# Output projection and first gate as plain products, and the rooms of SBUF in three zones

## The chip, the cores and the metric

The kernel runs on one core of one Trainium2 chip. The metric is the device time of one execution in microseconds; the median of three runs is shown below, and beside it one execution taken with the hardware profiler. The engines are TensorE (PE; its weight loads are PEld), VectorE (DVE), ScalarE (ACT), GpSimd (POOL) and SyncE (SP, which issues most DMAs). Each works through its own queue in order and waits on semaphores for the others.

## The reference

A decoder of two layers on one sequence of 1024 tokens, model width 1024, all in float32. Cut to what matters here:

```python
for i in range(DEPTH):                                  # 2 layers
    u = rms_norm(h, attn_norm_w[i])
    proj = u @ w_in[i]                                  # all heads' inputs
    fox = forgetting_attention(...)                     # 8 heads of 64, causal softmax with forget gates
    ret = silu(rg) * head_group_norm(chunkwise_retention(...))   # 8 heads of 64
    mixed = jnp.concatenate([fox, ret], axis=-1)
    h = h + mixed @ w_out[i]                            # output projection, 1024 x 1024
    h = h + gated_conv_ffn(rms_norm(h, ffn_norm_w[i]), w_up[i], conv_w[i], conv_b[i], w_down[i])
    gate = jax.nn.sigmoid(rms_norm(h, ple_norm_w[i]) @ w_ple_gate[i])   # gate, 1024 x 1024
    h = h + gate * (p[i] @ w_ple_proj[i])
return rms_norm(h, final_norm_w)
```

## The kernel before, in words

Activations lie with features on the 128 partitions and the 1024 tokens along the free axis, so a vector of 1024 features is eight tiles of 128x1024. A float32 product is made of three passes on TensorE: every operand is split into a high part (a cast to fp32r) and a low part (the rest), and high x high, low x high and high x low are summed in PSUM. ScalarE casts the high part (`wh`, `xh`, `dh`, `uh`), VectorE or GpSimd subtracts for the low one (`wl`, `xl`, `dl`, `ul`).

There are two ways to multiply. The *plain* one (`dense_fm`) makes one block of 128 output features from eight tiles of 128 input features: 8 x 3 x 2 matmuls of 128x512, 48 in all, and one result `d` of 128x1024. The *seven-product* one (`g_parts`) treats 256 inputs by 256 outputs by two halves of the tokens as a 2x2 block product and makes it with seven products where eight would be needed (names `b0 c1 b1 c2 b2 a b3`). For it the weights are combined: `Fixed` loads two raw tiles `wr`, GpSimd adds them to `ws`, ScalarE and VectorE split them in four stages. The moving side is combined too: `Joined` makes four stages (`x`, `xh`, `xl`) from two tiles with VectorE's help (`t2`, `t34`). Each of the seven results is added to its quarter by `join` (sums into h) or `form` (new tiles). `Line` keeps one set of weights in preparation while the one before is used: after parts 0, 2, 4 and 6 one step of the next is issued. The second and later parts of `b` and `c` go into the same PSUM bank on top of the first, after the first has been read.

The program of a layer: the input projections of the heads are plain. `weave` mixes their steps with units of attention by the numbers in `SPANS` (position at which a unit starts and should end, in microseconds of dense work); four pairs of fox heads come first, then four pairs of retention heads. The dense work in order is `DENSE`; its last entry `wo0` (`g_out`) is the first half of the output projection, that of the fox heads, beside the last retention unit. When all units are done the second half follows, then the up projection with convolution (11 bodies, each two `g_parts` a and z), the down projection (four groups), and the gate. In layer 0 the output projection, up, down and gate use seven products; the gate of layer 1 is plain. h goes to DRAM between stages and comes back by DMA. Plain weights come through `weight_order`, `fetch` and `weights`, one set ahead, and `load_w` splits them on the engine that `ENGINES` names.

All large tiles live in one arena of 50 rooms of 128x1024 and 6 of half the size. `take` gives the room that has been free longest, `back` puts it at the end of the queue; a new holder's first write must wait until the old holder's last reader is done. The order of instructions on each engine is then set by a scheduler from these dependencies.

The lines shown in the profile as L145 are one helper through which every operation passes, so in the rows the names of tiles tell operations apart: `h<-h,d` is a join, `a` and `z` are the two results of an up body, `conv` its convolution, `sg` the gate.

Of the kernel before, what the change touches and what calls it, by code (L numbers as in the profile page):

```python
# [9 lines left out]
F32 = mybir.dt.float32  # L10
# [7 lines left out]
DEPTH = 2  # L18
# [17 lines left out]
DENSE = ("fi1", "rv0", "fi2", "fv1", "fi3", "ri0", "rv1", "rg0", "ri1", "ri2", "rg1", "ri3", "ep0", "em0", "wo0")  # L36
SPANS = ((6, 42.6), (42.6, 79.9), (85.9, 123.5), (130.4, 145.5), (138.9, 199.2), (194.7, 197.7), (217.3, 254.5), (251.1, 300.0))
# [3 lines left out]
ROOMS = 50  # L41
HALVES = 6
# [59 lines left out]
class Arena:  # L102


    def __init__(self, tc, pool, whole, half):
        self.tc, self.pool = tc, pool
        self.free = {T: deque("m%d" % i for i in range(whole)), T // 2: deque("n%d" % i for i in range(half))}
        self.taken = []
        self.first = {}

    def back(self, room):
        self.taken.remove(room.name)
        self.free[T if room.place[0] == "m" else T // 2].append(room.place)

    def take(self, name, dt, shape):
        free = self.free[T if int(np.prod(shape[1:])) > T // 2 else T // 2] or self.free[T]
        if not free:
# [42 lines left out]
def trunk(ctx, tc, ap):  # L160
# [4 lines left out]
    arena = Arena(tc, sb, ROOMS, HALVES)  # L165
# [43 lines left out]
    def weight_order():  # L209
        V, G_ = nc.vector, nc.gpsimd  # L210
        for l in range(DEPTH):
            qk = lambda j: (ap["wqk"][l, j], KC, P, E("qk", j))
            tm = lambda j: [(ap["wtm"][l, j, i], 4, 256, E("tm", 2 * j + i)) for i in range(2)]
            fv0 = [(ap["wfv"][l][:, a:b, :], b - a, FVW, G_) for a, b in FVK]
            specs = {"ep": lambda i: [], "wo": lambda i: [],
                     "fi": lambda i: [qk(i), qk(4 + i)], "fv": lambda i: tm(0), "ri": lambda i: [qk(8 + i), qk(12 + i)],
                     "rv": lambda i: tm(1 + i), "rg": lambda i: tm(3 + i),
                     "em": lambda i: [(ap["wproj"][l, j], 8, P, E("em", j)) for j in range(2)]}
# [693 lines left out]
    for l in range(DEPTH):  # L912
# [120 lines left out]
        def hand(now, then):  # L1033

            def after(n):
                for m in now:
                    m.drop(n)
                for m in then:
                    m.build(n)
            return after  # L1040

        def specs():
            for half in range(2):
                for q in range(4):
                    yield ap["wout"][l, half, q], 2
# [6 lines left out]
            if l + 1 < DEPTH:  # L1052
                for q in range(4):
                    yield ap["wgate"][l, q], 4

        def g_out():

            nonlocal line, u, rb
            u = rb = None
            del pr[:], ret_tab[:]  # L1060
            line = Line(specs())
            for p in range(2):
                mx.append(Joined(mixed[2 * p], mixed[2 * p + 1]))
                mixed[2 * p:2 * p + 2] = [None, None]
            for q in range(4):
                for m in (2 * q, 2 * q + 1):
                    h[m] = G("h")
                    nc.sync.dma_start(h[m], h_dram[m])
                to = h[2 * q:2 * q + 2]
                yield from g_parts(line, mx, lambda name, s: join(name, s, to))  # L1070

        fox_ops, ret_ops, ret_v, ret_tab, vst, tail = {}, {}, {}, [], [], []
        pr, mx, h, line = [], [], [None] * KC, None
        pp = dr.tile([KC, P, T], F32, name="pp")
        raw = []
        for name in ("qs", "ks"):
# [3 lines left out]
            if name == "qs":  # L1080
# [9 lines left out]
                  "em": lambda i: g_embed(), "wo": lambda i: g_out()}  # L1090
# [6 lines left out]
        del vst[:]  # L1097


        def scales(which, p):  # L1100
            return nw[:, which, 2 * p:2 * p + 1], nw[:, which, 2 * p + 1:2 * p + 2], minus[:, which, 2 * p + 1:2 * p + 2]

        stats = Stats()
        mx = [Joined(mixed[2 * p], mixed[2 * p + 1]) for p in (2, 3)]
        mixed = None
        u = []
        hs_dram = dr.tile([KC, P, T], F32, name="hs")
        for q in range(4):
            to = h[2 * q:2 * q + 2]
            parts(line, mx, lambda name, s: join(name, s, to), hand(mx, []) if q == 3 else None)  # L1110
            u.append(Joined(*to, scales(2 * NW_FFN + l, q)))
            for m in (2 * q, 2 * q + 1):
                stats.add(h[m], G("hsq"))
                nc.sync.dma_start(hs_dram[m], h[m])
                h[m] = None
        to = None
# [51 lines left out]
        for g, mx in enumerate(stored):  # L1168
            then = stored[g + 1] if g + 1 < len(stored) else []
            for q in range(4):  # L1170
# [9 lines left out]
                def after(n):  # L1180
                    for m in mx:
                        m.drop(n)
                    for m in then:
                        m.build(n)
                        if n < 3:
                            m.load(n + 1)
                    if not then and not ends:
                        u[2].build(n)
                parts(line, mx, lambda name, s: join(name, s, to), after if q == 3 else None)
                if not then:  # L1190
                    if ends:
                        u += [make_u(h[m], nw[:, 2 * NW_PLE + l, m:m + 1]) for m in (2 * q, 2 * q + 1)]
                    else:
                        u.append(Joined(*to, scales(2 * NW_PLE + l, q), q != 2))
                    for m in (2 * q, 2 * q + 1):
                        stats.add(h[m], G("hsq"), None, E("hsq", m))
                        if not ends:
                            nc.sync.dma_start(hs_dram[m], h[m])
                if not then and not ends:

                    for m in range(2 * q - 2 if q == 3 else 2 * q, 2 * q + 2):
                        if q != 2:
                            h[m] = None
# [3 lines left out]
        if not ends:  # L1207
            nstats = Stats()
            h_dram = dr.tile([KC, P, T], F32, name="hd")
            rb = None  # L1210
            old, u = u, []
            for q in range(4):
                sg = [G("sg") for i in range(2)]
                for m in (2 * q, 2 * q + 1):
                    h[m] = G("h")
                    nc.sync.dma_start(h[m], hs_dram[m])

                def scale_s(i):
                    nonlocal rb, stats
                    if rb is None:  # L1220
                        _, rb = stats.finish()
                        stats = None
                    return rb

                def after(n):
                    for m in old:
                        m.drop(n)
                    if n:
                        u.extend(make_u(h[m], nw[:, 2 * NW_ATTN + l + 1, m:m + 1]) for m in (2 * n - 2, 2 * n - 1))
                    if n == 2:  # L1230
                        fetch()
                parts(line, old, lambda name, s: form(name, s, sg, scale_s), after if q == 3 else None)
                for i in range(2):
                    m = 2 * q + i
                    pt = G("ppt")
                    nc.sync.dma_start(pt, pp[m])
                    nc.scalar.activation(sg[i], sg[i], AF.Sigmoid)
                    nc.gpsimd.tensor_tensor(sg[i], sg[i], pt, op=ALU.mult)
                    nc.vector.tensor_tensor(h[m], h[m], sg[i], op=ALU.add)
                    if q == 3:  # L1240
                        u.append(make_u(h[m], nw[:, 2 * NW_ATTN + l + 1, m:m + 1]))
                    nstats.add(h[m], sg[i])
                    nc.sync.dma_start(h_dram[m], h[m])
                    if q == 3:
                        h[m] = None
                sg = pt = None
            stats, nstats = nstats, None
            h = rb = old = None

    fetch()  # L1250
# [127 lines left out]
```

## Time and profile before

| what | value |
|---|---|
| median of 3 runs | 2899.47 us (2892.65 to 2899.89) |
| the profiled execution | 2898.59 us |
| its span (first to last instruction) | 2896.8 us |
| TensorE busy | 2717.5 us, 94%, 13718 matmul records |
| VectorE busy | 2086.6 us, 72% |
| ScalarE busy | 1226.5 us, 42% |
| GpSimd busy | 902.0 us, 31% |
| mean granted TensorE clock | 0.970 |

A record is one matmul instruction as the profiler saw it; a float32 matmul that isn't split has two. Matmuls overlap, so the mean duration of one (about 400 ns) isn't the time it takes out of the stream; the distance from one to the next is. Busy shares over the whole span mix stages that different engines limit, so the tables by stretches matter more.

### The profile page before, as it was taken

The page shows a single profiled execution, that of the slowest core. Times are in us where ns is not written, and L with a number is a line of the kernel's source. Part 1 is how long each engine was busy: PE and PEld are TensorE (multiplying, and loading weights), DVE is VectorE, ACT ScalarE, POOL GpSimd, SP SyncE. Part 2 cuts the span into 40 slices and gives each one's busy share as a digit, 9 for nine tenths or more (in the row PEclk, how much of TensorE's full clock was granted, in tenths as well). Part 3 has the DMA queues.
Part 4 walks back from the last instruction along what each step waited for, and adds up shares of the span by engine and source line. Part 5 has one row for each costly group of instructions (what it writes and reads, how often), then busy time and mean ns, then how long its engine had stood idle before and what let it go on. Part 6 is the DMA issues. An engine that isn't in the chain of part 4 may idle for free. (4 is left out here: it accounts for less than half of the span.)

```text
span 2896.8 us, 36327 instructions
## 1 busy us (share of the span) xinstructions
PE 2717.5 (94%) x13718; PEld 2263.5 (78%) x13718; DVE 2086.6 (72%) x3031; ACT 1226.5 (42%) x1824; POOL 902.0 (31%) x652
## 2 busy tenths in 40 slices
PE   8988999978999998997889989999799999989998
PEld 7887989757888887775678879897578888867776
DVE  4565645898887778779745556458978877787786
ACT  4354543444344333435434545424443433434352
POOL 3222332223233323434432222322232333234240
PEclk9999999999999999998989999999999999999999
DMA  5333122422323236433533331224223232364242
GB/s 161 88 81 95 54 61 71 158 76 95 109 99 113 95 132 213 153 95 120 178 91 88 81 97 52 62 72 154 77 95 109 99 112 96 137 208 151 87 146 98
DMA packets 116864, 315.77 MB, mean 109 GB/s; under 512 B 13520, under 2 KB 34512, under 8 KB 116688
## 3 DMA queue, kind: packets, MB, share of 16 engines
q1 hardware_dynamic: 113616, 305.05, 32.4%
q10 hardware_dynamic: 3072, 8.39, 1.2%
q8 instruction: 108, 1.77, 0.3%
q14 instruction: 68, 0.56, 0.1%
HBM read 210.04 MB, written 69.80 MB: 97 GB/s over the span
## 5 line engine op out<-in xcount | busy, mean ns | idle before, releaser
L145 POOL TENSOR_TENSOR ws<-wr 128x512 f32<-128x512 f32 (+2 forms) x192 | 285.7, 1495 | 1049.6 <-PE d L145 520.6
L145 PE MATMUL s<-xh,wh 128*128 128x512 f32 x936 | 377.8, 406 | 25.6 <-ACT wh L145 13.2
L145 PE MATMUL d<-xh,wh 128*128 128x512 f32 x936 | 374.8, 404 | 20.2 <-DVE h L145 12.6
L145 PE MATMUL s<-xl,wh 128*128 128x512 f32 x936 | 377.4, 403 | 11.2 <-DVE xl L145 11.2
L145 PE MATMUL s<-xh,wl 128*128 128x512 f32 x936 | 372.0, 403 | 6.1 <-DVE wl L145 5.7
L145 PE MATMUL d<-xl,wh 128*128 128x512 f32 x936 | 373.6, 399 | 2.4 <-DVE xl L145 2.4
L145 PE MATMUL d<-xh,wl 128*128 128x512 f32 x936 | 370.6, 399 | 0.0
L145 POOL TENSOR_TENSOR ws<-ws,wr 128x512 f32<-128x512 f32 (+2 forms) x192 | 262.9, 1370 | 104.2 <-issue 55.6
L145 PE MATMUL d<-x,w 128*128 128x512 f32 x936 | 246.2, 399 | 22.4 <-ACT x L145 8.8
L145 ACT CAST wh<-ws 128x1024 fp32r<-128x1024 f32 (+2 forms) x192 | 168.5, 888 | 219.8 <-POOL ws L145 203.6
L145 DVE TENSOR_TENSOR wl<-ws,wh 128x1024 fp32r<-128x1024 f32 (+2 forms) x192 | 218.3, 1146 | 40.7 <-ACT wh L145 31.9
L145 PE MATMUL d<-dh,uh 128*128 128x256 f32 (+1 forms) x768 | 222.1, 290 | 22.8 <-DVE vst L145 11.2
L145 PEld LDWEIGHTS s<-xh,wh 128*128 128x128 f32 x936 | 180.0, 192 | 76.3 <-ACT wh L145 20.5
L145 PEld LDWEIGHTS d<-xh,wh 128*128 128x128 f32 x936 | 178.9, 191 | 71.5 <-DVE h L145 21.0
L145 PEld LDWEIGHTS d<-x,w 128*128 128x128 f32 x936 | 175.3, 190 | 71.1 <-ACT x L145 10.1
L145 PEld LDWEIGHTS s<-xl,wh 128*128 128x128 f32 x936 | 180.5, 193 | 54.8 <-DVE xl L145 14.3
L145 PEld LDWEIGHTS s<-xh,wl 128*128 128x128 f32 x936 | 180.0, 192 | 54.5 <-DVE wl L145 13.3
L145 PE MATMUL d<-dl,uh 128*128 128x256 f32 (+1 forms) x768 | 221.8, 289 | 0.0
L145 PE MATMUL d<-dh,ul 128*128 128x256 f32 (+1 forms) x768 | 220.8, 288 | 0.0
L145 PE MATMUL d<-uh,dh 128*128 128x512 f32 (+1 forms) x584 | 197.6, 407 | 18.1 <-ACT dh L145 11.1
L145 PEld LDWEIGHTS d<-xl,wh 128*128 128x128 f32 x936 | 179.6, 192 | 43.7 <-DVE xl L145 3.0
L145 PEld LDWEIGHTS d<-xh,wl 128*128 128x128 f32 x936 | 178.9, 191 | 42.2
(209 smaller groups left out, 5863.3 us busy)
## 6 DMA issues: line engine op xcount, KB each, us to landing
wr<-in_wup_dram SPq DMA_DIRECT2D x88, 512.0 KB, 3.8
zz<-zd SPq DMA_DIRECT2D x66, 512.0 KB, 3.7
wr<-in_wdown_dram SPq DMA_DIRECT2D x48, 384.0 KB, 4.2
zd<-z SPq DMA_DIRECT2D x66, 256.0 KB, 2.0
dr<-in_wqk_dram SPq DMA_DIRECT2D x32, 512.0 KB, 3.5
hs<-h SPq DMA_DIRECT2D x24, 512.0 KB, 2.6
h<-hs SPq DMA_DIRECT2D x24, 512.0 KB, 4.8
zd<-t SPq DMA_DIRECT2D x22, 512.0 KB, 3.9
```

The source lines that it names most:

```text
L145: ins = f(*[bare(v) for v in a], **{n: bare(v) for n, v in k.items()})
```

## The change

The output projection of both layers and the gate of layer 0 become plain: one block of 128 outputs after the other with `dense_fm`, from weights in a plain layout that `weight_order` now delivers (`wout`, `wgate`). All eight tiles of mixed are split once, after the weave; no part of the projection is left in the weave, so the last retention unit ends at position 259.3 instead of 300. The moving sides of the up projection are still `Joined`, made after every second block. The next layer's moving sides are made in the gate, block by block. The arena has zones: 28 rooms for moving sides, 9 for split weights, 13 for the rest, 6 halves; a tile looks in its own zone first, then in r, w, x.

```diff
-DENSE = (... "ri3", "ep0", "em0", "wo0")
-SPANS = (... (217.3, 254.5), (251.1, 300.0))
+DENSE = (... "ri3", "ep0", "em0")
+SPANS = (... (217.3, 254.5), (251.1, 259.3))
-ROOMS = 50
-HALVES = 6
+ZONES = dict(x=28, w=9, r=13, n=6)
+HOMES = dict(x=("x", "xh", "xl", "uh", "ul", "mxh", "mxl", "qq", "ka", "kb"), w=("w", "wh", "wl", "dh", "dl"))
...
     def take(self, name, dt, shape):
-        free = self.free[T if int(np.prod(shape[1:])) > T // 2 else T // 2] or self.free[T]
+        home = next((z for z, names in HOMES.items() if name in names), "r")
+        zones = [home] + [z for z in "rwx" if z != home]
+        if int(np.prod(shape[1:])) <= T // 2:
+            zones.insert(0, "n")
+        free = next((self.free[z] for z in zones if self.free[z]), None)
...
+            yield from [(ap["wout"][l, m], KC, P, E("wo", m)) for m in range(KC)]
             yield None
-            for i in range(len(PIECES) if l + 1 == DEPTH else 0):
-                yield from [(ap["wlast"][0, m], KC, P, E("gate%d" % l, i * KC + m)) for m in range(KC)]
+            for i in range(len(PIECES) if l + 1 == DEPTH else 1):
+                yield from [(ap["wgate"][l, m], KC, P, E("gate%d" % l, i * KC + m)) for m in range(KC)]
...
+        mx = []
+        for c in range(8):
+            mx.append((G("mxh", F32R), G("mxl", F32R)))
+            split(*mx[c], mixed[c], E("mx", c))
+            mixed[c] = None
...
-        for q in range(4):
-            to = h[2 * q:2 * q + 2]
-            parts(line, mx, lambda name, s: join(name, s, to), hand(mx, []) if q == 3 else None)
-            u.append(Joined(*to, scales(2 * NW_FFN + l, q)))
...
+        for m in range(KC):
+            h[m] = G("h")
+            nc.sync.dma_start(h[m], h_dram[m])
+            if m == 4:
+                line = Line(specs())
+            elif m > 4:
+                line.step()
+            d = dense_fm(weights(), mx)
+            nc.vector.tensor_tensor(h[m], d, h[m], op=ALU.add)
+            nc.sync.dma_start(hs_dram[m], h[m])
+            stats.add(h[m], G("hsq"))
+            if m % 2:
+                u.append(Joined(h[m - 1], h[m], ...))
...
-                parts(line, old, lambda name, s: form(name, s, sg, scale_s), after if q == 3 else None)
+            for m in range(KC):
+                pt = G("ppt")
+                nc.sync.dma_start(pt, pp[m])
+                d = dense_fm(weights(), u)
+                if m == 0:
+                    _, rb = stats.finish()
+                sg = G("sg")
+                if m < 2:
+                    nc.scalar.copy(sg, d)
+                nc.vector.tensor_tensor(sg, sg if m < 2 else d, rb, op=ALU.mult)
+                nc.scalar.activation(sg, sg, AF.Sigmoid)
+                nc.vector.tensor_tensor(sg, sg, pt, op=ALU.mult)
+                nc.vector.tensor_tensor(h[m], h[m], sg, op=ALU.add)
+                then.append(make_u(h[m], nw[:, 2 * NW_ATTN + l + 1, m:m + 1]))
+                nstats.add(h[m], sg)
```

TensorE at the end of layer 0's attention, where the last retention unit is turned (`s<-ident,yn`). Before, seven-product matmuls of the output projection (`x,w`, `xh,wh`) stand around it:

```order
L145 MATMUL d<-x,w 128x512 x2
L145 MATMUL s<-xh,wh 128x512
L145 MATMUL s<-xl,wh 128x512
L145 MATMUL s<-ident,yn 128x128 x4
L145 MATMUL d<-x,w 128x512 x4
L145 MATMUL d<-xh,wh 128x512
L145 MATMUL d<-xl,wh 128x512
L145 MATMUL s<-xh,wl 128x512
```

After, products of the embedding (`ph`, `pl`) stand ahead of it, and the plain projection (`mxh`, `mxl`) begins behind it:

```order
L154 MATMUL d<-ph,dh 128x512 x2
L154 MATMUL d<-pl,dh 128x512 x2
L154 MATMUL d<-ph,dl 128x512 x2
L154 MATMUL s<-ident,yn 128x128 x4
L154 MATMUL d<-mxh,dh 128x512 x2
L154 MATMUL d<-mxl,dh 128x512 x2
L154 MATMUL d<-mxh,dl 128x512 x2
```

The output projection has moved behind the whole of the retention.

ScalarE in one body of the up projection of layer 0. Before, the result of c1 (`z<-s`) is read between the two first passes of the convolutions (`conv<-a,convp`):

```order
L145 COPY z<-d 128x512
L145 ACTIVATE conv<-a,convp 128x1024
L145 CAST w<-wr 128x512
L145 ACTIVATE z<-s 128x512
L145 ACTIVATE conv<-conv 128x1024
L145 CAST wh<-ws 128x1024
L145 ACTIVATE conv<-a,convp 128x1024
L145 CAST wh<-ws 128x1024
L145 COPY z<-d 128x512
```

After, it is read behind both of them, and behind the second `z<-d`:

```order
L154 ACTIVATE conv<-a,convp 128x1024
L154 CAST wh<-wr 128x1024
L154 ACTIVATE conv<-conv 128x1024
L154 COPY z<-d 128x512
L154 ACTIVATE conv<-a,convp 128x1024
L154 CAST w<-wr 128x512
L154 COPY z<-d 128x512
L154 ACTIVATE conv<-conv 128x1024
L154 ACTIVATE z<-s 128x512
```

`z<-s` has moved behind the second convolution's first pass and the first one's Gelu.

VectorE where layer 0's output projection ends. Before, joins (`h<-h,d`, `h<-h,s`) alternate with the last moving side of the up projection (`t_6303`, `t_6304`, `x`, `xl`):

```order
L145 TENSOR_TENSOR h<-h,d 128x512
L145 TENSOR_TENSOR xl<-t_6193,xh 128x512
L145 SCALAR_TENSOR_TENSOR t_6303<-h,nw,t_6304 128x512
L145 SCALAR_TENSOR_TENSOR x<-h,nw,x 128x512
L145 TENSOR_TENSOR ssq<-ssq,hsq 128x1024
L145 SCALAR_TENSOR_TENSOR xl<-h,nw,xh 128x512
L145 SCALAR_TENSOR_TENSOR t_6303<-h,minus,t_6303 128x512
L145 SCALAR_TENSOR_TENSOR t_6304<-h,nw,t_6304 128x512
L145 TENSOR_TENSOR wl<-ws,wh 128x1024
L145 TENSOR_TENSOR h<-h,d 128x512
L145 TENSOR_TENSOR wl<-ws,wh 128x1024
```

After, one sum (`h<-d,h`) for the last block precedes the same work (`t_6127`, `t_6128`):

```order
L154 TENSOR_TENSOR h<-d,h 128x1024
L154 SCALAR_TENSOR_TENSOR x<-h,nw,x 128x512
L154 TENSOR_TENSOR ssq<-ssq,hsq 128x1024
L154 SCALAR_TENSOR_TENSOR xl<-h,nw,xh 128x512 x2
L154 SCALAR_TENSOR_TENSOR t_6127<-h,nw,t_6128 128x512
L154 SCALAR_TENSOR_TENSOR t_6127<-h,minus,t_6127 128x512
L154 SCALAR_TENSOR_TENSOR t_6128<-h,nw,t_6128 128x512
L154 TENSOR_SCALAR rc<-s 128x8
L154 SCALAR_TENSOR_TENSOR t_6128<-h,minus,t_6127 128x512
L154 TENSOR_TENSOR xl<-t_6127,xh 128x1024
L154 TENSOR_TENSOR xl<-t_6128,xh 128x512 x2
```

The joins are gone; the chain from the last sum to the last `xl` has stayed.

## Rows read from the trace of the kernel before

**Rows 1.** The page: span, shares of two engines, granted clock in 40 slices.
```profile
span 2896.8 us, 36327 instructions
...
PE 2717.5 (94%) x13718; PEld 2263.5 (78%) x13718; DVE 2086.6 (72%) x3031; ACT 1226.5 (42%) x1824; POOL 902.0 (31%) x652
...
PEclk9999999999999999998989999999999999999999
```

**Rows 2.** Busy time by stretches, first line the columns (x counts records).
```profile
core 0: us, PE busy (x) PEld busy (x) DVE busy (x) ACT busy (x) POOL busy (x), PEclk, DMA share, GB/s
590.00:690.00 100.00, 78.37 (x301) 57.47 (x300) 91.01 (x122) 50.11 (x72) 33.89 (x26) 0.90 0.25 88
620.00:680.00 60.00, 43.59 (x150) 31.53 (x149) 60.00 (x77) 33.31 (x47) 17.63 (x13) 0.86 0.32 114
2040.00:2140.00 100.00, 78.34 (x303) 58.15 (x302) 89.69 (x120) 50.61 (x73) 32.66 (x26) 0.90 0.25 90
1300.00:1460.00 160.00, 129.60 (x501) 98.22 (x500) 134.50 (x142) 80.92 (x103) 71.14 (x38) 0.89 0.41 145
700.00:1090.00 390.00, 390.00 (x1685) 315.81 (x1684) 308.76 (x304) 153.23 (x187) 121.88 (x78) 1.00 0.32 112
2810.00:2850.00 40.00, 40.00 (x175) 32.46 (x174) 31.87 (x41) 17.94 (x26) 4.86 (x2) 1.00 0.26 85
2750.00:2800.00 50.00, 46.34 (x190) 34.71 (x189) 48.21 (x50) 28.87 (x34) 24.91 (x15) 1.00 0.38 127
440.00:460.00 20.00, 18.04 (x137) 17.18 (x136) 18.40 (x29) 4.35 (x6) 10.40 (x4) 0.96 0.20 60
```

**Rows 3.** Costliest groups of TensorE from 590 to 690 us, the narrow ones (busy us, mean ns).
```profile
L145 PE MATMUL s<-ones,ssq 128*128 128x1 f32 x16 | 1.8, 245 | 0.0
L145 PE MATMUL s<-ident,rc 128*128 128x128 f32 x11 | 1.4, 275 | 0.0
L145 PE MATMUL s<-ident,yn 128*128 128x128 f32 x8 | 1.2, 275 | 1.8 <-DVE yn L145 1.8
```

**Rows 4.** Timeline of TensorE, waits in two transitions (start us, us, ..., idle before, releaser).
```profile
654.18 2.34 PE L145 MATMUL d<-x,w 128*128 128x512 f32 x9 [2.30 <-DVE h L145]
...
662.91 0.58 PE L145 MATMUL d<-x,w 128*128 128x512 f32 x1 [4.08 <-ACT x L145]
...
1447.34 0.80 PE L145 MATMUL d<-xh,wh 128*128 128x512 f32 x1 [5.38 <-DVE sg L145]
...
1458.57 1.22 PE L145 MATMUL d<-ul,dh 128*128 128x512 f32 x2 [5.75 <-DVE ul L145]
```

**Rows 5.** Costliest groups of VectorE from 590 to 690 us.
```profile
L145 DVE TENSOR_TENSOR h<-h,d 128x512 f32<-128x512 f32 x18 | 12.0, 676 | 0.7 <-PE d L145 0.7
L145 DVE TENSOR_TENSOR ssq<-ssq,hsq 128x1024 f32<-128x1024 f32 x7 | 8.5, 1212 | 0.0
L145 DVE TENSOR_TENSOR xl<-t,xh 128x1024 fp32r<-128x1024 f32 x6 | 8.0, 1339 | 0.0
```

**Rows 6.** Costliest groups over the whole span, plain weight splits on VectorE.
```profile
L145 DVE TENSOR_TENSOR dl<-dr,dh 128x1024 fp32r<-128x1024 f32 x27 | 42.2, 1565 | 33.8 <-ACT dh L145 21.1 <-issue 12.7
```

**Rows 7.** Timeline of ScalarE and VectorE in one up body.
```profile
812.84 0.60 ACT L145 ACTIVATE z<-s 128x512 f32<-128x512 f32 x1
...
817.19 1.25 ACT L145 ACTIVATE conv<-a,convp 128x1024 f32<-128x1024 f32 x1 [0.63 <-DVE a L145]
...
809.97 2.60 DVE L145 SCALAR_TENSOR_TENSOR conv<-a,convp,conv 128x1023 f32<-128x1023 f32 x2
...
818.72 3.63 DVE L145 SCALAR_TENSOR_TENSOR conv<-a,convp,conv 128x1023 f32<-128x1023 f32 x2
```

**Rows 8.** Timeline of GpSimd and VectorE in the gate of layer 0.
```profile
1429.41 5.77 POOL L145 TENSOR_TENSOR sg<-sg,ppt 128x1024 f32<-128x1024 f32 x2 [11.97 <-ACT sg L145]
...
1432.82 3.44 DVE L145 TENSOR_TENSOR h<-h,sg 128x1024 f32<-128x1024 f32 x1
```

More of the change, by code (lines that the diff above doesn't have):

```diff
@@ L102, with __init__ @@
 class Arena:
-    def __init__(self, tc, pool, whole, half):
+    def __init__(self, tc, pool):
         self.tc, self.pool = tc, pool
-        self.free = {T: deque("m%d" % i for i in range(whole)), T // 2: deque("n%d" % i for i in range(half))}
+        self.free = {z: deque("%s%d" % (z, i) for i in range(n)) for z, n in ZONES.items()}
         self.taken = []
         self.first = {}
+        for places in self.free.values():
+            for place in places:
+                pool.tile([P, T // 2 if place[0] == "n" else T], F32, name="room", tag=place, bufs=1)
     def back(self, room):
         self.taken.remove(room.name)
-        self.free[T if room.place[0] == "m" else T // 2].append(room.place)
+        self.free[room.place[0]].append(room.place)
     def take(self, name, dt, shape):
-        free = self.free[T if int(np.prod(shape[1:])) > T // 2 else T // 2] or self.free[T]
-        if not free:
+        home = next((z for z, names in HOMES.items() if name in names), "r")
[3 more added lines that the diff above has]
+        free = next((self.free[z] for z in zones if self.free[z]), None)
+        if free is None:
             raise MemoryError("no room left for %s: %s" % (name, ", ".join(sorted(self.taken))))
@@ L1031, in ret @@
             return g_retention(*ret_ops.pop(pair), v, lambda: ret_v["rg"][pair], mixed[4 + pair], tail)
[L1033 to L1040, printed above, removed]
         def specs():
-            for half in range(2):
-                for q in range(4):
-                    yield ap["wout"][l, half, q], 2
             for j in range(FC // 2):
@@ L1051, in specs @@
                     yield ap["wdown"][l, q][:, :, :, group[0] * P:(group[-1] + 1) * P], len(group)
[L1052 to L1068, printed above, removed]
-                to = h[2 * q:2 * q + 2]
-                yield from g_parts(line, mx, lambda name, s: join(name, s, to))
         fox_ops, ret_ops, ret_v, ret_tab, vst, tail = {}, {}, {}, [], [], []
-        pr, mx, h, line = [], [], [None] * KC, None
+        pr, h = [], [None] * KC
         pp = dr.tile([KC, P, T], F32, name="pp")
@@ L1096, in trunk @@
         ret_v.clear()
-        del vst[:]
-        def scales(which, p):
-            return nw[:, which, 2 * p:2 * p + 1], nw[:, which, 2 * p + 1:2 * p + 2], minus[:, which, 2 * p + 1:2 * p + 2]
+        del vst[:], pr[:], ret_tab[:]
+        u = rb = None
+        mx = []
[3 more added lines that the diff above has]
+            mixed[c] = None
+        mixed = None
         stats = Stats()
-        mx = [Joined(mixed[2 * p], mixed[2 * p + 1]) for p in (2, 3)]
-        mixed = None
+        hs_dram = dr.tile([KC, P, T], F32, name="hs")
         u = []
-        hs_dram = dr.tile([KC, P, T], F32, name="hs")
-        for q in range(4):
-            to = h[2 * q:2 * q + 2]
-            parts(line, mx, lambda name, s: join(name, s, to), hand(mx, []) if q == 3 else None)
-            u.append(Joined(*to, scales(2 * NW_FFN + l, q)))
[L1112 to L1116, printed above, removed]
+        for m in range(KC):
[6 more added lines that the diff above has]
+            d = dense_fm(weights(), mx)
+            if m == KC - 1:
+                mx = None
+            nc.vector.tensor_tensor(h[m], d, h[m], op=ALU.add)
+            nc.sync.dma_start(hs_dram[m], h[m])
+            stats.add(h[m], G("hsq"))
+            if m % 2:
+                s1 = slice(m - 1, m)
+                s2 = slice(m, m + 1)
+                u.append(Joined(h[m - 1], h[m], (nw[:, 2 * NW_FFN + l, s1], nw[:, 2 * NW_FFN + l, s2], minus[:, 2 * NW_FFN + l, s2])))
+                h[m - 1:m + 1] = [None, None]
         zd = [dr.tile([4, P, T], F32, name="zd%d" % j, bufs=1) for j in range(FC // 2)]
@@ L1186, in after @@
                             m.load(n + 1)
-                    if not then and not ends:
-                        u[2].build(n)
                 parts(line, mx, lambda name, s: join(name, s, to), after if q == 3 else None)
                 if not then:
[L1191 to L1194, printed above, removed]
+                    u += [make_u(h[m], nw[:, 2 * NW_PLE + l, m:m + 1]) for m in (2 * q, 2 * q + 1)]
                     for m in (2 * q, 2 * q + 1):
                         stats.add(h[m], G("hsq"), None, E("hsq", m))
[L1197 to L1203, printed above, removed]
+                    if q == 2:
+                        fetch()
         mx = then = stored = to = None
@@ L1247, in trunk @@
-            stats, nstats = nstats, None
-            h = rb = old = None
-    fetch()
+            then = []
+            for m in range(KC):
[4 more added lines that the diff above has]
+                    _, rb = stats.finish()
+                    stats = None
+                sg = G("sg")
[7 more added lines that the diff above has]
+                nstats.add(h[m], sg)
+                nc.sync.dma_start(h_dram[m], h[m])
+                h[m] = None
@@ L1253, in final_norm @@
+            u, then, stats, nstats = then, None, nstats, None
+            h = rb = pt = sg = None
     def final_norm(pstats, at, c):
```

49 lines of the change are left out of this document (7 added, 42 removed).

## The prediction

> **What bounds the kernel now.** I read the page first, for the share of each engine [rows 1]: TensorE is busy 2717.5 of 2896.8 us and VectorE 2086.6, and the line of the granted clock is 9 in all but two of 40 slices, so TensorE is the bound on the average. An average over stages hides the rest, so the next view was the table by stretches, one row for each stage [rows 2]. The reader is to compare two things in it: how many matmuls a stretch holds, and which engine fills it. In the stretch from 700 to 1090 us, the up projection of layer 0, TensorE is busy 390.00 of 390.00 us with 1685 records: 390.00 / 1685 = 231.5 ns for one 128x512 matmul of the seven-product form, with nothing left to gain. In the plain gate of layer 1 (2810 to 2850) it is 40.00 / 175 = 228.6 ns. These two are my prices of a matmul. At 231.5 ns the 301 records between 590 and 690 us, the end of layer 0's output projection, are worth 69.7 us of the 100 that pass; 35 of them are narrow and take 4.4 us together [rows 3], so the work is 266 x 0.2315 + 4.4 = 66.0 us and 34 us are lost. The same place of layer 1 (2040 to 2140) has 303 records: 70.1 us, 29.9 lost, 34 with the same allowance for narrow ones. From 1300 to 1460, the end of the down projection and the gate of layer 0, 501 records are worth 116.0 of 160 us: 44 lost, some 46 with a somewhat smaller allowance. That is 34 + 34 + 46 = 114 us, and the granted clock is 0.89 to 0.90 there against 1.00 in the full stretches, which is a part of the same loss, not another one.
>
> What fills these stretches instead is VectorE: 91.01 of 100, 89.69 of 100, 134.50 of 160 us, and from 620 to 680 us 60.00 of 60.00 [rows 2]. The timeline of TensorE names it at the waits [rows 4]: 2.30 us for h (a sum on VectorE), 4.08 us for x (made from the last h), and in the gate 5.38 us for sg and 5.75 us for ul. So in three places of the program the bound is VectorE, which joins seven products, splits the weights of each combination and forms the moving sides.
>
> **The change, part by part.** *Matmuls.* One seven-product stage has 336 wide matmuls, the plain one 384. Each of the three stages goes from 336 x 0.2315 = 77.8 us to 384 x 0.2286 = 87.8 us, so 10.0 us more, 30 us in all, if TensorE runs without a gap.
>
> *VectorE in the output projection.* Before, each layer joins 8 x 7 = 56 products of 128x512 at 676 ns [rows 5]: 38 us. After, eight sums of 128x1024; the nearest rows are two halves at 676 ns and a 128x1024 operation at 1212 ns [rows 5], so 1.2 to 1.4 us each, 10 to 11 us. That alone takes 27 us off VectorE in each layer; the four-stage splits of four pairs of mixed and of eight sets of combined weights go too, and eight plain weight splits come, at 1565 ns where VectorE does them [rows 6], and eight plain splits of mixed, of which four go to GpSimd. For two blocks of columns (96 matmuls, 21.9 us of TensorE) VectorE then has two sums (2.6), two weight splits (3.1), two sums of squares (2.4) and the moving side for the up projection, some ten operations between 0.7 and 1.34 us (the longest of them in [rows 5]), about 9 us: 17 of 21.9 us. In the last three blocks some 5 us of up weights are added, still inside 32.9 us. So TensorE becomes the bound of the stage and the 34 us shrink to its two ends. At its start, the last retention unit has lost the projection of the fox heads as its filler; only 48 matmuls of the embedding are there, and the order keeps 36 of them for the last group norm. The nearest row is a stretch in which another unit runs almost bare, 440 to 460 us: TensorE is busy 18.04 of 20 us at a clock of 0.96 [rows 2]. I take 5 us for a unit and its tail, bounds 2 and 15. At its end, the last sum must pass before the up projection can have its last pair: sum 1.3, first split 0.7 + 0.8, sum of squares 1.2, two splits 1.6, four scaled differences 3.2, cast 1.05, difference 1.34, together 11.2 us; the order gives TensorE 24 ready matmuls (5.6 us) to do meanwhile, so 6 us of idling. That is 11 us left in each layer.
>
> *Gate of layer 0.* The down projection now hands over to plain moving sides, as it does today in layer 1: from 2750 to 2800 us 190 records are worth 44.0 of 50 us [rows 2], so 6 us are lost. The first two columns wait for the norm (2 us), and at the end the last column needs product, sigmoid, product, sum and a split (about 7.5 us) while the next layer's first dense block has seven of its eight steps ready (42 x 0.2286 = 9.6 us): 0 to 5 us, I take 4. So 12 us stay of 46. The product with ppt moves from GpSimd to VectorE, eight times 1.2 us, inside 87.8 us of TensorE; h is kept and not read again.
>
> One more row of that place: VectorE's sum of h and sg takes 3.44 us at 1432.82 while GpSimd runs two products from 1429.41 for 5.77 us [rows 8], against 1.21 us of a like operation [rows 5]. The Trainium skill (SBUF — State Buffer, SBUF: two separate sides) says that VectorE with two inputs in SBUF and GpSimd hold one port pair by turns, for a whole instruction. The trace agrees. By this rule the four splits of mixed on GpSimd would hold up VectorE at the end of retention, by at most their own length.
>
> I price that from the row as well: GpSimd splits of this size are at most 2.9 us (5.77 / 2), four in a layer, mostly beside transposes that don't need VectorE: 0 to 8 us in a layer, inside the bounds of the 5 us above.
>
> *The zones.* 50 rooms stay 50, but a tile now takes one from its own zone first, so the up projection turns over in the 22 rooms of two zones and gets rooms that have only just been left. In the order on ScalarE the evacuation of the second product into z (z<-s) stands before the second convolution in the kernel before, and behind it now, because z takes the rooms of a. In the trace that evacuation is at 812.84 us, and the convolution's last tap on VectorE ends at 818.72 + 3.63 = 822.35 [rows 7], 9.5 us later. The next product that adds to the same bank waits for it. But VectorE can be earlier: after the last product of a it has one product for a (0.7), two or three weight splits (1.2 to 1.34, as the operations of that size in [rows 5]), four taps (2.60 / 2 to 3.63 / 2) and two other operations, 11.4 to 13 us, and TensorE has four parts of twelve matmuls to do until then, 48 x 0.2315 = 11.1 us. So 0.3 to 1.9 us in those bodies where the room of the second a is taken, about every second of 22: 3 to 21 us, and nothing if VectorE runs ahead. I take 8 us. Bounds: 0 and 22 x 6.7 = 147 us (9.5 less one part of 2.8 us as cover). In the attention stages the short reuse follows TensorE's own order (the new writer needs a later product of TensorE anyway): 0, bounds -10 and +15. The weights of the last gate are fetched earlier; that hides under the down projection: 0.
>
> **The sum.** -114 + (11 + 11 + 12) + 30 + 8 = -42 us. Against the profiled execution's own time of 2898.6 us that is 2856.6; the median of the runs is 0.9 us above that time, so I say 2857.
>
> **Rivals.** *The rooms bind (slower).* If VectorE stays as late as in the trace, each of the 22 up bodies waits; from 50 / 22 = 2.3 us a body the gain is gone, at 4 us it is 2898.6 - 50 + 88 = 2937. For it: z behind the second convolution in the order. Against it: VectorE is busy 308.76 of 390 us there [rows 2], so 8.1 us of a body of 39 us are free to catch up. The Trainium skill (Perfetto Trace Analysis, Identifying Performance Opportunities) says that the same gap repeated on the engine that should be full can mean too little SBUF for the next tile; no gap repeats in this trace between 700 and 1090 us, and the rule would show itself in just this rival. Chance 0.14.
> *TensorE is the bound after all (slower).* The transitions lose what they lose now, since they hang on chains and not on VectorE's load, and 30 + 8 us are added: 2937. Against it: 60.00 of 60.00 us. Chance 0.04.
> *Half.* Retention bare costs its 15 us in each layer and the up bodies 1 us each: 2857 + 20 + 14 = 2891; with one of the two 2875. Chance 0.22.
> *More.* The ends hide wholly and the rooms cost nothing: 2857 - 34 = 2823. Chance 0.14.
> *No effect* that can be told, gain and loss cancelling: 0.03. The forecast itself, 2845 to 2870: 0.43.
>
> **How the numbers follow.** About 0.3% (8.7 us) can be told from no change. Faster: forecast, more, and most of half, 0.43 + 0.14 + 0.20 = 0.77. Same: 0.03 and the slow edge of half, 0.05. Slower: 0.18. Leaving out a third of *more* and most of the two slower rivals, the range is 2822 to 2908; the likeliest case's own range is 2842 to 2872.
>
> **What would show it.** Right: in the profile after, TensorE near 44 matmuls in 10 us all through the three plain stages, VectorE below 85% there, and one idle time of 5 to 8 us where the up projection begins. Right on the zones: the first up body stretches still 390 of 390. Wrong: gaps of TensorE before d or s in every up body, released by ScalarE's z or VectorE's conv; or a retention tail of more than 15 us with the clock at its lower level of 1.2 GHz; or VectorE again at 90% in the plain stages.

## The result: 3010 us, 3.8% slower than before

| | before | changed |
|---|---|---|
| median of the runs | 2897.24 us (2892.65 to 2899.89, 4 runs) | 3009.89 us (3004.08 to 3013.12, 4 runs) |
| ratio | 1 | 1.0382, 95% interval 1.0368 to 1.0397 |
| the profiled execution / its span | 2898.59 / 2896.8 us | 3010.55 / 3008.3 us |

The forecast was 2857 us, the range 2822 to 2908. The page of the changed kernel, the lines that answer to [rows 1]:

```profile
span 3008.3 us, 36022 instructions
...
PE 2752.9 (92%) x13862; PEld 2302.5 (77%) x13862; DVE 1914.3 (64%) x2760; ACT 1166.6 (39%) x1702; POOL 815.0 (27%) x579
...
PEclk9999999999999999999989999999999999999998
```

TensorE has more to do (2752.9 against 2717.5 us), VectorE 172 us less, but the span has grown by 111.5 us: what came is neither work nor a fuller engine, but waiting. The stretches of the changed kernel that answer to [rows 2], with its columns:

```profile
570.00:670.00 100.00, 96.97 (x432) 79.26 (x430) 56.50 (x62) 37.84 (x48) 12.07 (x7) 1.00 0.41 142
2075.00:2175.00 100.00, 94.82 (x423) 78.27 (x423) 60.22 (x68) 36.74 (x47) 9.72 (x8) 0.98 0.38 137
1350.00:1510.00 160.00, 143.21 (x635) 116.35 (x636) 99.73 (x94) 62.04 (x66) 34.41 (x20) 0.96 0.28 93
700.00:1090.00 390.00, 360.01 (x1500) 284.78 (x1498) 274.85 (x273) 137.66 (x166) 117.78 (x72) 0.97 0.28 95
828.70:832.50 3.80, 3.80 (x10) 2.98 (x11) 3.63 (x5) 1.75 (x2) 0.00 (x0) 0.55 0.01 2
835.50:850.00 14.50, 14.50 (x66) 12.01 (x65) 8.27 (x9) 3.65 (x4) 4.04 (x3) 1.00 0.13 50
```

The first two are the output projections. There the forecast came true: VectorE has fallen from 91.01 and 89.69 of 100 us to 56.50 and 60.22, and TensorE has 432 and 423 records where it had 301 and 303. The third is the end of the down projection with the gate, VectorE 99.73 of 160 us; its 635 records are only 39.7 in 10 us, since TensorE waits 13.18 us there for a cast of weights (e6 comes back to it). The largest loss is in the fourth, the up projection that was full: 360.01 of 390 us and 1500 records, against 390.00 and 1685. The last two lines are for the section on hardware.

The starts of three kinds of rows in VectorE's timeline (a layer's first convolution tap, its last convolution row, `conv<-conv,rb`, and the last sum of h and sg in each gate) cut the span into six pieces, which serve for all runs below (us; e1 to e12 are the experiments, 0 and 1 the layers):

| kernel | start to first tap 0 | up 0 | to end of gate 0 | to first tap 1 | up 1 | to the end |
|---|---|---|---|---|---|---|
| before | 699.2 | 405.9 | 358.6 | 682.8 | 405.4 | 330.7 |
| changed | 696.8 | 452.5 | 348.6 | 697.4 | 449.5 | 350.5 |
| e1 one queue | 681.9 | 401.1 | 326.5 | 658.3 | 400.3 | 337.1 |
| e2 before, zones | 718.6 | 436.7 | 356.1 | 697.6 | 438.6 | 344.8 |
| e3 mixed in r | 708.8 | 427.9 | 353.1 | 704.2 | 429.3 | 350.2 |
| e4 z in x | 697.2 | 432.7 | 347.8 | 695.2 | 436.3 | 351.8 |
| e5 last freed first | 727.3 | 530.1 | 415.9 | 705.6 | 536.5 | 433.9 |
| e6 dr in x | 694.6 | 454.3 | 333.5 | 676.8 | 453.2 | 337.1 |
| e7 before, plain gate | 698.0 | 406.0 | 330.3 | 679.7 | 405.9 | 340.8 |
| e8 e1, late last fetch | 680.3 | 400.4 | 326.7 | 658.7 | 401.1 | 324.3 |
| e9 17 rooms | 673.7 | 410.2 | 329.5 | 652.8 | 410.0 | 337.1 |
| e10 15 rooms | 673.7 | 416.8 | 332.5 | 650.7 | 417.2 | 339.9 |
| e11 before, rooms first | 697.8 | 399.6 | 356.3 | 681.7 | 397.5 | 327.0 |
| e12 e8, rooms late | 680.2 | 409.1 | 329.3 | 660.8 | 409.0 | 330.8 |

Two places show in the trace how the zones cost time; what they cost in all is measured by e1. In the up projection of the changed kernel (timelines of VectorE, ScalarE, GpSimd and TensorE, in brackets the idle time before and its releaser):

```profile
817.79 2.00 DVE L154 TENSOR_TENSOR wl<-ws,wh 128x1024 fp32r<-128x1024 f32 x1 [2.77 <-ACT wh L154]
...
825.71 1.28 DVE L154 SCALAR_TENSOR_TENSOR conv<-a,convp,conv 128x1022 f32<-128x1022 f32 x1
...
827.09 1.06 ACT L154 ACTIVATE conv<-conv 128x1024 f32<-128x1024 f32 x1 [1.47 <-DVE conv L154]
...
828.05 0.57 ACT L154 COPY z<-d 128x512 f32<-128x512 f32 x1
...
828.67 0.72 PE L154 MATMUL d<-xh,wh 128*128 128x512 f32 x1 [2.27 <-ACT z L154]
...
863.07 3.00 POOL L154 TENSOR_TENSOR ws<-wr 128x512 f32<-128x512 f32 x2 [15.71 <-DMA wr<-in_wup_dram]
...
866.02 3.60 POOL L154 TENSOR_TENSOR ws<-ws,wr 128x512 f32<-128x512 f32 x2
...
868.31 1.04 ACT L154 CAST wh<-ws 128x1024 fp32r<-128x1024 f32 x1 [3.40 <-POOL ws L154]
...
869.41 0.53 PE L154 MATMUL s<-xh,wh 128*128 128x512 f32 x1 [1.89 <-ACT wh L154]
```

The second to fifth lines: the last reader of a's room is the convolution's tap on VectorE, done at 826.99. z has been given that room, so its first write, z<-d, comes behind the tap and behind the Gelu that stands ahead of it in ScalarE's queue, at 828.05, and TensorE, which needs that bank of PSUM again, stands still for 2.27 us. VectorE is late with that tap, although it has idle time in every body: from 819 to 828 us it is busy 8.93 of 9.00 us, after 2.77 us in which it had to wait for the cast of a weight (first line).

Ten such waits of 2.1 to 2.3 us stand in TensorE's two up projections, one in two bodies. The last four lines: the raw weights wr, loaded into rooms that had only just come free (by the order of the program those of tiles t and z, whose copies to DRAM SyncE issues and waits for just before), reach GpSimd 15.71 us after its last work, and then sums, cast and split run in a row just ahead of TensorE (1.89 us).

At the start of layer 1's attention (SyncE's queue, ScalarE, TensorE):

```profile
1518.46 1.15 SPq L154 DMA_DIRECT2D qq<-qh  x2
...
1529.33 2.47 SPq L154 DMA_DIRECT2D dr<-in_wfv_dram  x2
...
1535.36 1.39 ACT L154 CAST dh<-dr 128x792 fp32r<-128x792 f32 x2 [15.54 <-DMA dr<-in_wfv_dram]
...
1536.26 0.81 PE L154 MATMUL d<-dh,uh 128*128 128x264 f32 x2 [17.38 <-ACT dh L154]
```

By the order of the program the two weight tiles dr of this fence have the rooms of qh and ql. Their loads must follow the copies out of these, which SyncE issues itself from 1518.46 on, and so they are issued at 1529.33, behind twelve other issues; the casts come at 1535.36, and TensorE has been idle for 17.38 us.

### The profile page after: what moved, and what is told of

Its sections match the earlier page's. It is cut to its first block, busy times and chain, and to the rows that moved or that the text cites. A ratio compares the mean times of both kernels' runs of the same rounds, so it can differ in the third digit from the quotient of the medians.

```text
span 3008.3 us, 36022 instructions
## 1 busy us (share of the span) xinstructions
PE 2752.9 (92%) x13862; PEld 2302.5 (77%) x13862; DVE 1914.3 (64%) x2760; ACT 1166.6 (39%) x1702; POOL 815.0 (27%) x579
## 5 line engine op out<-in xcount | busy, mean ns | idle before, releaser
L154 POOL TENSOR_TENSOR ws<-wr 128x512 f32<-128x512 f32 (+2 forms) x152 | 230.6, 1522 | 917.3 <-DMA wr<-in_wup_dram 314.8
L154 PE MATMUL d<-xh,wh 128*128 128x512 f32 x792 | 320.6, 405 | 37.1 <-ACT z L154 22.4
L154 PE MATMUL s<-xh,wh 128*128 128x512 f32 x792 | 315.3, 400 | 35.4 <-ACT wh L154 23.4
L154 PE MATMUL s<-xh,wl 128*128 128x512 f32 x792 | 310.1, 397 | 10.2 <-DVE wl L154 10.2
L154 PE MATMUL d<-xh,wl 128*128 128x512 f32 x792 | 316.4, 400 | 0.0
L154 PE MATMUL d<-xl,wh 128*128 128x512 f32 x792 | 316.4, 399 | 0.0
L154 PE MATMUL s<-xl,wh 128*128 128x512 f32 x792 | 312.9, 395 | 0.0
L154 POOL TENSOR_TENSOR dl<-dr,dh 128x1024 fp32r<-128x1024 f32 (+2 forms) x58 | 139.7, 2410 | 377.4 <-ACT dh L154 337.0
L154 PE MATMUL d<-uh,dl 128*128 128x512 f32 (+1 forms) x712 | 229.5, 394 | 3.6 <-POOL dl L154 3.5
L154 PE MATMUL d<-ul,dh 128*128 128x512 f32 (+1 forms) x712 | 229.9, 394 | 0.6 <-DVE ul L154 0.6
```

The source lines that it names most:

```text
L154: ins = f(*[bare(v) for v in a], **{n: bare(v) for n, v in k.items()})
```

## The experiments

Theory A: a room is written again straight behind its last reader, because a tile looks in its own zone first. Rivals: the plain stages and the bare last retention unit cost the time (B), or something else about the zones.

**e1: the zones undone.**

```diff
-ZONES = dict(x=28, w=9, r=13, n=6)
-HOMES = dict(x=("x", "xh", ...), w=("w", "wh", ...))
+ZONES = dict(r=50, n=6)
+HOMES = {}
...
```

> The changed kernel (plain output projection and first gate) with the 50 whole rooms in one queue again, as before; only the zones are undone. Theory A (the zones cost the time): the up bodies go back from 43.9 to 39.0 us (-91 us over both layers), the last stretch behind the second up projection from 355.6 to about 338 us (-18), and the plain stages then show what they are worth: 2855 to 2895 us, below the kernel before (2897). Rival B (the plain stages and the bare last retention unit cost the time, and the zones are innocent): 2980 to 3010 us, the up bodies still at 43 to 44 us.

Measured: 2819.5 us (2815.94 to 2821.72), ratio to before 0.9726 (0.971 to 0.9742). Theory A, and by more than it expected: the zones cost 190 us of the changed kernel, 100 in the two up projections and 90 elsewhere. TensorE's up projection is full again (columns as in [rows 2]):

```profile
720.00:1060.00 340.00, 340.00 (x1501) 281.53 (x1501) 276.14 (x269) 133.51 (x162) 111.10 (x71) 1.00 0.31 111
```

**e2: the zones alone**, put into the kernel before (its `Arena` replaced by the changed one).

> The kernel before (seven products everywhere) with the rooms in the three zones 28, 9, 13; only the zones are added. Theory A: the moving sides of the output projection fill the zone x when those of the up projection are built, so the latter spill into r and w here too, and the up bodies turn over in few rooms: 42 to 44 us a body, 2960 to 3010 us in all. Rival B (zones innocent): 2890 to 2905 us, bodies at 39.0.

Measured: 3010.7 us, ratio 1.0403 (1.0373 to 1.0433), just above the expected range, up projections 31 and 33 us longer, bodies of 42.3 and 42.8 us. B is out: no plain stage is in this kernel.

**e3 and e4: which tiles lie where.** e3 deletes `"mxh", "mxl"` from zone x's list, e4 adds `"z"` to it.

> The changed kernel with its zones, but mxh and mxl (the 16 split tiles of mixed) are taken out of the list of zone x, so that they start in r and w, and the 28 moving sides of the up projection all find a place in x. Theory A1 (what costs is that 9 of those 28 moving sides spill into r and w and stay there through the whole up projection, while rooms of x stand idle): all of r and w turn over in the up bodies, these go to 39 to 40 us, 2915 to 2940 us in all. Rival A2 (22 rooms of r and w are too few for an up body wherever the moving sides lie): bodies stay at 43 to 44 us and the time at 2990 to 3015.

Measured: 2994.32 us, ratio 1.0327 (1.0309 to 1.0346). The time is in the range of A2, the bodies, 41.7 us, lie between the two theories: the up projections win 25 and 20 us of the 51 and 49, and the start of both layers loses 12 and 7 us, where mxh and mxl now take rooms of r and w (that this is the reason wasn't shown). The edit does less than expected: followed through the code, 4 of the 28 moving sides still spill, since some of mxh and mxl overflow into x. So five spilled sides fewer bring back about half of the loss there, and A1 isn't tested to its end.

> The changed kernel with z added to the list of zone x, so that z takes one of the idle rooms of x and no longer the room that the first convolution still reads. Theory A (z in the room of a is the wait that counts most: 2.27 us every second body and about as much again at the lower clock behind it): 10 such gaps go, 2965 to 2975 us. Rival C (the weights are as late behind it: their rooms are left by the matmuls just before): another gap takes its place and the time stays above 2990.

Measured: 2981.21 us, ratio 1.0285 (1.0265 to 1.0305), between the two again. The wait for z has gone, and one for the weights stands in nearly every body in its place, 1.75 us, where 2.27 us for z and 1.9 for wh alternated (timeline of TensorE in e4):

```profile
795.60 0.50 PE L154 MATMUL s<-xh,wl 128*128 128x512 f32 x1 [1.75 <-DVE wl L154]
...
836.68 0.50 PE L154 MATMUL s<-xh,wl 128*128 128x512 f32 x1 [1.76 <-DVE wl L154]
```

**e5: one queue, the room freed last is taken first** (`free.pop()` for `free.popleft()` in e1).

> The changed kernel with one queue of 50 rooms, as in e1, but a new tile takes the room that came free last, not the one that has been free longest. No zones at all. Theory A (what costs is that a room is written again straight after its last reader): an up body turns over in 14 rooms instead of 21 and nearly every tile follows its predecessor at once, so it must be slower than with the zones: bodies of 46 us or more, over 3050 us. Rival D (the loss comes from something else that the zones bring, as the order into which the instructions fall, or how the rooms lie in SBUF): 2815 to 2850 us, since one queue has no zones.

Measured: 3365.09 us, ratio 1.1607 (1.158 to 1.1635): 546 us above e1 by the order of one queue. The age of the room is what counts, and zones aren't needed for the loss; that only 14 rooms turn over isn't the reason, since 15 with the oldest first take 2847 us (e10) (columns as in [rows 2]):

```profile
720.00:1060.00 340.00, 276.77 (x1088) 212.33 (x1087) 212.15 (x200) 103.74 (x122) 84.81 (x52) 0.94 0.22 74
```

**e6: `"dr"` added to zone x's list.**

> The changed kernel with its zones, with dr (raw plain weights as they come by DMA) added to the list of zone x. The up bodies have no dr, they stay at 43 to 44 us. Theory A (outside the up projections the zones cost time because the load of the next weights waits until the last reader of a room just left is done: the wait of 17.38 us at 1536 us, where dr takes the room of qh, which SyncE's own queue still reads): that wait goes, the one of 13.18 us in the gate shrinks, and the time is 2965 to 2985 us. Rival E (those waits are waits for the DMA itself or for the norm, wherever dr lies): 3000 to 3012 us.

Measured: 2958.02 us, ratio 1.0199 (1.0172 to 1.0226), 52 us below the changed kernel; the up projections are as long as there, and the gain is in the gate, the attention of layer 1 and the last gate (15, 21 and 13 us). The load no longer waits for the copies of qh; ScalarE's cast stands ahead of qh's now, and at the place of the 13.18 us in the gate TensorE waits 1.47 us (last line):

```profile
1477.59 0.86 ACT L154 CAST dh<-dr 128x792 fp32r<-128x792 f32 x1 [4.41 <-DMA dr<-in_wfv_dram]
...
1503.80 1.05 ACT L154 CAST qh<-qs 128x1024 fp32r<-128x1024 f32 x1
...
1422.19 0.73 PE L154 MATMUL d<-uh,dh 128*128 128x512 f32 x2 [1.47 <-ACT sg L154]
```

**e7: the plain gate alone** (the kernel before with the changed kernel's gate of layer 0).

> The kernel before (one queue, output projection by seven products) with the gate of layer 0 alone as plain products: one part of the change by itself. By the prediction's sum -46 + 12 + 10 = -24 us: 2873 to 2880 us. If instead the whole of what e1 gained between the first up projection and the end of the gate belongs to it, -37 us: 2860 to 2866. Rival B (the gate's plain form brings nothing, the loss is a wait for the norm): 2895 to 2910.

Measured: 2880.92 us, ratio 0.9936 (0.9914 to 0.9959). The piece with the gate is 28.3 us shorter (forecast 24), the last piece 10 us longer.

**e8: e1, and the last gate's first weights fetched late, as before.**

```diff
-                    if q == 2:
+                    if q == 2 and not ends:
                         fetch()
...
+    fetch()
     def final_norm(pstats, at, c):
```

> e1 (plain stages, one queue) with the first weights of the last gate fetched behind the down projection again, as in the kernel before, and not at its third step; the gate of layer 0 keeps the early fetch. In e1 and e7 TensorE waits 4.5 us for rc (GpSimd) in the last gate and the time from the last convolution to the last sum is 337 and 341 us, in the kernel before 0.9 us and 331. If the early fetch does that: 2810 to 2815 us. If it is something else: 2817 to 2822, as e1 (2819.5).

Measured: 2807.95 us (2804.16 to 2810.24), ratio 0.9688 (0.9674 to 0.9701). The early fetch costs 11.6 us. TensorE in the last gate, first e1, then e8:

```profile
2725.09 3.78 PE L154 MATMUL s<-ident,rc 128*128 128x128 f32 x16 [4.58 <-POOL rc L154]
```

```profile
2714.29 2.05 PE L154 MATMUL s<-ident,rc 128*128 128x128 f32 x16 [0.94 <-POOL rc L154]
```

This version beats both kernels.

**e9 and e10: fewer rooms in one queue.** `kept = [G("kept") for _ in range(4)]` (six in e10) ahead of e1's up projection, given back in its tenth body.

> e1 with four of the 50 rooms held empty through the up projection, so that 17 rooms turn over there in one queue instead of 21. Theory F (the number of rooms that turn over sets the wait, whatever zone they belong to): e3 also turns over in 17 and has bodies of 41.5 us against 38.05 in e1, so bodies of 41 to 42 us and 2875 to 2900 us in all. Rival G (a queue needs fewer rooms than zones with fixed homes, since every tile gets the oldest): bodies below 39.5 us, 2819 to 2850 us.

> e1 with six rooms held empty through the up projection: 15 rooms turn over in one queue. Theory F: between e3 (17 rooms, 41.5 us a body) and the changed kernel (13 rooms of r and w beside overflow into x, 43.6 us): 42.5 to 43.5 us a body, 2910 to 2935 us. Rival G: below 41 us a body, under 2885 us.

Measured: 2832.22 us, ratio 0.9774 (0.9761 to 0.9788), and 2847.16 us, 0.9822 (0.9808 to 0.9836). My theory F fell. With the 17 rooms of e3 in one queue the up projection takes 410 us, in e3 428; with 15 rooms it takes 417, with 21 (e1) 401. So the number of rooms explains 9 of the 27 us that e3 loses there. The other 18 go with the zones, where by the code a tile takes the oldest room of its own zone even while one left earlier lies free in another; no run tests this step by itself (columns as in [rows 2], e3 first, then e9):

```profile
720.00:1060.00 340.00, 321.75 (x1370) 256.57 (x1368) 254.31 (x247) 123.73 (x149) 105.79 (x65) 0.99 0.30 99
```

```profile
720.00:1060.00 340.00, 334.91 (x1454) 270.17 (x1453) 264.37 (x262) 126.19 (x156) 112.17 (x70) 1.00 0.31 106
```

**e11 and e12: where the rooms lie.** A full up projection has 340 / 1501 = 226.5 ns from matmul to matmul in e1, against 231.5 in the kernel before. The zones' code also lays out all rooms at the start; e11 does only that in the kernel before, e12 takes it from e8.

```diff
+        for n, places in self.free.items():
+            for place in places:
+                pool.tile([P, n], F32, name="room", tag=place, bufs=1)
```

> The kernel before with one thing of the change: all rooms are laid out in SBUF at the start, one behind the other, and not each when it is first taken. Where TensorE is full, one wide matmul follows the other after 231.5 ns in the kernel before and in e7 (rooms laid out late), after 226.7 to 227.8 ns in the changed kernel and in e1 to e6 and e8 to e10 (rooms laid out first). Theory H (it is the layout): 227 ns here too; some 5500 wide matmuls of the seven-product stages at 4.6 ns less are 25 us, as much as 40 with the plain ones: 2857 to 2875 us. Rival I (the spacing goes with something else, as the plain output projection or the zones): 231.5 ns and 2893 to 2902 us.

> The kernel of e8 (plain stages, one queue, late last fetch) with each room laid out when it is first taken, as in the kernel before. Theory H: 231.5 ns from matmul to matmul in the up projection, and 2830 to 2850 us instead of 2808. What is then left against the kernel before is the worth of the plain stages alone, -50 us by the prediction without its term for the zones. Rival I: 227 ns, 2804 to 2812 us.

Measured: e11 2872.77 us, ratio 0.9916 (0.9899 to 0.9932), e12 2837.3 us, 0.9794 (0.978 to 0.9809). Theory H in both (columns as in [rows 2], e11, then e12):

```profile
720.00:1060.00 340.00, 340.00 (x1502) 281.70 (x1501) 276.74 (x267) 135.29 (x162) 113.71 (x71) 1.00 0.30 108
```

```profile
720.00:1060.00 340.00, 340.00 (x1469) 275.69 (x1468) 269.77 (x261) 130.31 (x157) 109.99 (x71) 1.00 0.30 107
```

TensorE is full in both and its clock 1.00: 1502 records against 1469, 226.4 ns against 231.4. In both pairs (the kernel before and e11, e8 and e12) the traces show the same instructions in the same order on TensorE, VectorE, ScalarE and GpSimd, so no difference in the work stands behind the spacing.

## Why the prediction was wrong

The runs split the change in four: plain stages -58.5 us (e12, 2837.3 against 2895.8), rooms laid out first -29.4 (e8 against e12), early last fetch +11.6 (e1 against e8), zones +190.4 (the changed kernel against e1). These are steps along one chain of kernels, so their sum, +114, has to come out at the measured +112.7 but for the drift of the kernel before from round to round; it is no proof of the split. In another order the parts can differ: in the kernel before the zones cost 138 us (e2 against e11).

- *The plain stages, right.* The prediction's -114 + 34 + 30 = -50 us were measured as -58.5. Its output projection, -34 + 11 + 10 = -13 us in each layer, came out at -14.7 and -15.8 (e12 against e7, start of the layer to the last convolution row), its gate, -24, at -28.3 (e7). The 6 us of idling that it saw where the up projection begins are 1.93 us in e12 (at 663.58 us, for xl). That the stages hung on VectorE's load holds, and the rival "TensorE is the bound after all" falls with it.
- *The zones, the step that failed.* The prediction says "the up projection turns over in the 22 rooms of two zones" and "I take 8 us". It cost 100 us there. The step counted 22 rooms, but following `take` through the code, the 16 tiles mxh and mxl still hold x when the 28 moving sides of the up projection are made, so 9 of those spill into r and w and stay there to the end. 13 rooms were left, one of them held by the norm's factor rb, while the rooms that mxh and mxl left in x served as overflow alone: by the order of the program no matmul lies between the last reader of the first z's room and the product that z takes over, in one queue 48 do. The wait expected at z<-s came at z<-d, longer than the 0.3 to 1.9 us of the prediction, and it was one of several: the waits for the weights (1.9 us) have no term in the sum, and e4 shows that they take the place of the one for z. The rival "the rooms bind" had the place and the sign, and the prediction's list of signs the tell-tale ("gaps of TensorE before d or s ... released by ScalarE's z"); at its 4 us a body it gave 2937. The trace has 5.8: 8 bodies from the wait for z at 739.62 us to that at 1090.45, 43.85 each, against 38.08 in e1 (from tap to tap).
- *The zones in the attention and the gates*: "the short reuse follows TensorE's own order ...: 0, bounds -10 and +15". It cost 90 us. The new writer isn't always behind TensorE: it can be a load, which waits in SyncE's queue for readers in that same queue. e6 shows 49 us of it; the rest wasn't taken apart.
- *The fetch*: "that hides under the down projection: 0" was +11.6 us. With it TensorE waits 4.58 instead of 0.94 us for rc, and the granted clock around it is 0.87 (e1, 2700 to 2740 us) instead of 1.00 (e8, 2690 to 2730), some 5 us more by an estimate from these two. Why the order of one fetch moves rc wasn't followed.
- *The layout of the rooms* wasn't in the sum: -29.4 us here, -23 in the kernel before (e11).
- *The range.* The upper bound for the zones in the up projections, 147 us, was worked out and then left outside the range, on the strength of 8.1 us that VectorE had free in a body. That was a mean. VectorE was late at the wait for z, busy 8.93 of 9.00 us from 819 to 828, after it had waited 2.77 us for a cast of weights on ScalarE. *More* was summed wrongly besides: without the 34 us of the ends and the 8 of the rooms it is 2815, not 2823.

One rule that the prediction weighed can be told again now. The Trainium skill (Perfetto Trace Analysis, Identifying Performance Opportunities) says that one gap recurring on the engine that ought to be full may mean too little buffer space for the next tile. The trace agrees about the gap, with 2.27 us in every second body and 1.75 in nearly every one of e4, but the space as a whole was not too small: with four rooms fewer and the oldest first (e9) TensorE has no wait above 1.2 us from 715 to 1060 us.

Open in part: why the zones cost less in the kernel before (138 us, e2 against e11) than in the changed one. By the table most of the difference stands in the gate of layer 0 (0 against 22 us) and the start of layer 1 (16 against 39), where moving dr won 15 and 21 us in e6; nothing of e2 was taken apart.

## What to carry to other kernels

Give a tile the room that has been free longest over the whole arena. Where zones are wanted, follow the allocator through the code for each zone: what still lies in it when the next stage's long-lived tiles are made, and where these spill. For each reuse ask on which queue the new first writer waits and what stands behind it there; a load on the queue that issues the old tile's copies is the worst case seen here (17.38 us). Test an allocator by itself before it is joined to a change of the arithmetic: here one hid a gain of 58 us from the plain stages in a loss of 113.

## What the runs showed of the hardware

- A short wait can cost more than itself. In the stretch from 828.70 to 832.50 us, right behind the wait of 2.27 us, the granted clock is 0.55, near the lower of its two levels (1.2 of 2.4 GHz), and 10 matmuls are recorded in 3.80 us; from 835.50 it is 1.00 again, 66 in 14.50. At 0.22 us each the ten would have taken 2.2 us, so the wait cost 2.27 + 1.6 us. It isn't so behind every wait: behind the one of 1.75 us in e4 (at 795.60 us) the clock stays at 1.00, with 19 records in 4.40 us (columns as in [rows 2]). My prediction priced waits at their length.

```profile
795.60:800.00 4.40, 4.40 (x19) 3.63 (x20) 4.12 (x6) 1.36 (x3) 0.00 (x0) 1.00 0.73 245
```

- Where the rooms lie in SBUF changes the pace of matmuls at full clock: 226.4 against 231.4 ns (e11, e12), 2%, with TensorE busy 340.00 of 340.00 us in both and the same order of instructions. Which property of the addresses does it wasn't tried.
